# Preparing a chunked RWKV-7 scan: products of one engine given to another, and decays read one column to the left

## The chip, the cores and the metric

One NeuronCore of a Trainium2 chip runs the whole program in one launch. Its engines work side by side, each through its own queue in order: TensorE (PE, matrix products), VectorE (DVE), ScalarE (ACT), GpSimd (POOL) and SyncE (SP), which only issues the transfers here. An instruction waits at the head of its queue until the semaphores it names are reached. The metric is the device time of one execution in microseconds (us), as the median of a few runs.

## The reference, cut to what matters

The program computes two blocks. The first is a modulated norm, an input projection, two mixers (retention and RWKV-7, both run forward and backward over time), an output projection and a mixture of 16 experts; the second has two layers of attention-like mixers and a feed-forward part. The change touches only the preparation of the RWKV-7 scan of the first block, for 256 tokens and 256 context tokens, eight heads of 64 channels:

```
def decay(wl, w0_d, w2_d):
    w_log = -jax.nn.softplus(-(w0_d + jnp.tanh(wl) @ w2_d)) - 0.5
    return heads(jnp.exp(-jnp.exp(w_log)))
iclr = jax.nn.sigmoid(a0 + al @ a2)
kk = heads(k * k_k)
kk = kk / jnp.maximum(jnp.linalg.norm(kk, axis=-1, keepdims=True), 1e-12)
k_mod = heads(k * (1.0 + (iclr - 1.0) * k_a))
...
    sa = jnp.einsum('bhvk,bhk->bhv', S, a_t)
    S = S * w_t[:, :, None, :] + sa[..., None] * b_t[:, :, None, :] + v_t[..., None] * k_t[:, :, None, :]
    return S, jnp.einsum('bhvk,bhk->bhv', S, r_t)
```

with `a = -kk` and `b = kk * iclr`.

## The kernel before, in words

**The scan in chunks.** The kernel takes the scan in chunks of 64 tokens. In a chunk the decays become running products, so the kernel sums their logarithms along the chunk (`pf`, a scan on DVE, L678), takes exponentials of the sums on ACT, and multiplies keys, rates and read vectors with them. The results are two kinds of tiles: `AX` (what is read: `a` and `r` with their decay) and `BK` (what is written: `k` and `b` with the inverse decay). Both exist for `part` 1 (context) and `part` 0 (tokens), in the order's names `ax1`/`ax0` and `bk1`/`bk0`; which pair of channel blocks they belong to is told by a number. Channels come in four blocks `b` of 128; directions are `d`.

**`rwkv_decay`** (L665 to L687) runs twice with two blocks each: for b = 0 and 1 at 131 to 150 us, for b = 2 and 3 at 207 to 226 us. For each direction it computes the log decay `lw` (ACT L676, DVE L677), its running sum `pf` (DVE L678), on GpSimd the sum without a token's own decay, `lw = pf - lw` (L679), and five exponentials on ACT (L685 to L687), some of `pf` and some of the new `lw`. All the exponentials of one direction stand in one row on the ACT queue, and behind the last of them stand the roundings `wh` (L346) of the next weights of the input projection.

**Weights.** The projection runs in three passes per weight tile `w`: ACT rounds it to `wh` (L346), DVE computes the rest `wl = w - wh` (L348, every twelfth piece on POOL), and PE multiplies both. So PE waits for ACT and DVE where these two are busy with something else.

**`rwkv_prep`** (L690 to L750) computes, for one block, the normed key `av` (the last step is L726), the tile `KB` that holds `b` and the modified key (L730 on POOL for the head e = 0 and on DVE for e = 1), the bonus (L734, L738), and then multiplies the exponentials in place: `AX` by `av` (L744), `BK` by `KB` (L748) and `AX`'s second row by the read vector `rc` (L750). For part 1 the first two are on DVE, for part 0 on POOL; L750 is always on POOL. Two blocks are woven with each other and with the projection that gives the next blocks' inputs: b = 0, 1 at 228 to 262 us (round 1), b = 2, 3 at 262 to 298 us (round 2). `AF.Ln` (L711) and the functions `Exp` and `Tanh` (L719, L702) need different tables of ACT, hence the table loads.

**After that** come the scores (`rwkv_scores`, which begin with ACT L779), the inverse of a triangular matrix for the context, all on DVE (`rwkv_inverse` with `part` 1, L823 and L825), and the one for the tokens on POOL. Of the 32 scores of the tokens, the first 16 are masked on POOL (`mask`, L1346), while DVE works on the first inverse. `R.marks` holds DVE's instructions of that inverse, in order. Then come the scan's steps, the output projection and the experts, whose weights SP begins to fetch as soon as tiles of the steps are free (L1594, L1617).

The order of each queue is made when the program is built: the instructions are written by hand in interleaved generators (`weave`), and a scheduler with modelled durations picks the order, `later` giving some a delay and `issue_after` naming an instruction behind which others may be picked.

Of the kernel before, what the change touches and what calls it, by code (L numbers as in the profile page):

```python
# [11 lines left out]
AF = mybir.ActivationFunctionType  # L12
OP = mybir.AluOpType
AX = mybir.AxisListType
# [242 lines left out]
LY = 200  # L257
VM = [(1, 3, 5, 7), (1, 3, 5, 7)]
M1 = 20
NM = 16  # L260
LOW = 17
PLAN = "40044420644644006046040420666,26425,0,42,0,,,,140,1005,100,,10,,,303,3,,31,,,,3,3,3530"
# [4 lines left out]
class K:  # L267
# [39 lines left out]
    def col(s, n, i=None):  # L307
        o, w = s.at["col"][n]
        return s.colt[:, o:o + w] if i is None else s.colt[:, o + i:o + i + 1]
# [111 lines left out]
def ch(a):  # L421
    return a.rearrange("p (c t) -> p c t", t=64)


def hsl(h):
    return slice(64 * (h % 2), 64 * (h % 2) + 64)


def c64(h):
    return slice(64 * h, 64 * h + 64)  # L430


def c128(i):
    return slice(128 * i, 128 * i + 128)
# [133 lines left out]
def later(k, n):  # L568

    return k.tc.high_priority(offset=-n)  # L570
# [28 lines left out]
def weave(*gens):  # L599

    gens = list(gens)
    while gens:
        for g in list(gens):
            if next(g, gens) is gens:
                gens.remove(g)
# [33 lines left out]
def rwkv_in(k, R, bb, hT, m, own=None):  # L639

    S = k.S
    n, cw = ((512, "cw_k"), (1024, "cw_v"), (0, "cw_r"))[m]
    w = wcols(k, RW + n + 256 * bb)
    nt = 256 if m == 2 else 512
    for b in range(2):
        p = dense_t(k, w, 128 * b, 128, hT, nt)
        x = own[:, nt * b:nt * b + nt] if own is not None else k.t([128, nt], *(None, k.tq, ("rc", 2))[m])
        conv3(k, p, cw, 2 * bb + b, x)  # L650
        if m == 1:
            if bb == b == 1:
                yield
            with later(k, LC):
                p = k.ps("pr")
                for j in range(4):
                    k.mm(p[:, c128(j)], x[:, c128(j)], k.tab("cen"))
                S.activation(R.v[:, :, c128(2 * bb + b)], p.rearrange("p (j n) -> p j n", j=4), AF.Copy)
                p = k.ps("pr")
                for i in range(2):  # L660
                    k.mm(p[:, 2 * i:2 * i + 2], x[:, c128(i)], k.tab("hsel"))
                S.activation(R.mean[:, :, 4 * bb + 2 * b:4 * bb + 2 * b + 2],
                             p[:, :4].rearrange("p (i c) -> p i c", i=2), AF.Copy, scale=1.0 / 64)
        yield x


def rwkv_decay(k, R, b):

    V, G, S = k.V, k.G, k.S
    pt = lambda a, part: ch(a[:, 256 * part:256 * part + 256])  # L670
    ps = [k.ps("pr") for _ in range(2)]
    k.beside(*[(ps[d], R.w2[c64(d), c128(b)], R.wl[c64(d), :]) for d in range(2)])
    for d in range(2):
        p = ps[d]
        lw, pf = k.t([128, 512], *k.tq), k.t([128, 512], *k.tq)
        S.activation(lw, p, AF.Tanh, scale=0.5, bias=R.hw[:, 4 * d + b:4 * d + b + 1])  # L676
        V.tensor_scalar(lw, lw, -0.5 * DECAY, -0.5 * DECAY, op0=OP.mult, op1=OP.add)  # L677
        V.tensor_tensor_scan(pf, R.rs, lw, 0.0, op0=OP.mult, op1=OP.add)  # L678
        G.tensor_tensor(lw, pf, lw, op=OP.subtract)  # L679
        S.activation(R.WC[:, d, :, b], ch(pf)[:, :, 63], AF.Exp)  # L680

        fa, fb, sg = (lw, pf, 1.0) if d == 0 else (pf, lw, -1.0)
        for part in (1, 0):
            AX, BK = R.AX[part][b // 2][:, d, b % 2], R.BK[part][b // 2][:, d, b % 2]
            S.activation(AX[:, :, 0, :], pt(fa, part), AF.Exp, scale=sg)  # L685
            S.activation(BK, pt(fb, part)[:, :, None, :].to_broadcast([128, 4, 2, 64]), AF.Exp, scale=-sg)
        S.activation(R.AX[0][b // 2][:, d, b % 2, :, 1, :], pt(fb, 0), AF.Exp, scale=sg)  # L687


def rwkv_prep(k, R, b, kc, rc):  # L690


    V, G, S, col = k.V, k.G, k.S, k.col
    q2 = lambda n=512: k.t([128, 512], *k.tq)[:, :n]
    bs = c128(b)
    pt = lambda a, part: ch(a[:, 256 * part:256 * part + 256])

    with later(k, LP):
        p = k.ps("pr")
        k.mm(p, R.a2[:, bs], R.al)  # L700
        thi = q2()
        S.activation(thi, p, AF.Tanh, scale=0.5, bias=R.hw[:, 8 + b:9 + b])  # L702
    with later(k, LQ):
        rn = q2()
        S.activation(rn, kc, AF.Square, scale=col("k_k", b))
        p = k.ps("pr")
        k.mm(p, k.tab("bones"), rn)
    yield
    with later(k, LQ):
        V.tensor_scalar(rn, p, 1e-24, None, op0=OP.max)  # L710
    S.activation(rn, rn, AF.Ln)  # L711
    km = q2()
    if AC & 1:
        S.activation(km, thi, AF.Identity, scale=R.ka[:, b:b + 1], bias=R.ka[:, 4 + b:5 + b])
    else:
        V.tensor_scalar(km, thi, R.ka[:, b:b + 1], R.ka[:, 4 + b:5 + b], op0=OP.mult, op1=OP.add)
    V.tensor_tensor(km, km, kc, op=OP.mult)
    yield
    S.activation(rn, rn, AF.Exp, scale=-0.5)  # L719
    if AC & 2:  # L720
        S.activation(thi, thi, AF.Copy, scale=-0.5, bias=-0.5)
    else:
        V.tensor_scalar(thi, thi, -0.5, -0.5, op0=OP.mult, op1=OP.add)
    yield
    av = rn
    V.scalar_tensor_tensor(av, kc, R.ka[:, 8 + b:9 + b], rn, op0=OP.mult, op1=OP.mult)  # L726
    yield
    KB = k.t([128, 8, 2, 64], "kb", 2)
    for e in range(2):
        (G, V)[e].tensor_tensor(KB[hsl(e), :, e, :], ch(thi)[hsl(e)], ch(av)[hsl(e)], op=OP.mult)  # L730
        S.activation(KB[hsl(e), :, 1 - e, :], ch(km)[hsl(e)], AF.Copy)
    yield
    pr = q2(256)
    V.scalar_tensor_tensor(pr, rc, col("r_k", b), km[:, :256], op0=OP.mult, op1=OP.mult)  # L734
    p = k.ps("py")
    for i in range(2):
        k.mm(p[:, 2 * i:2 * i + 2], pr[:, c128(i)], k.tab("hsel"))
    V.tensor_copy(R.bonus[:, :, 2 * b:2 * b + 2], p[:, :4].rearrange("p (i c) -> p i c", i=2))  # L738
    for part, E in ((1, V), (0, G)):
        for d in range(2):  # L740
            yield
            AX, BK = R.AX[part][b // 2][:, d, b % 2], R.BK[part][b // 2][:, d, b % 2]
            x = AX[:, :, 0, :]
            E.tensor_tensor(x, x, pt(av, part), op=OP.mult)  # L744
            S.activation(AX[hsl(1), :, 2 - part, :], x[hsl(1)], AF.Copy)
            if part:
                G.memset(x[hsl(1)], 0.0)
            E.tensor_tensor(BK, BK, KB[:, 4 * part:4 * part + 4], op=OP.mult)  # L748
            if part == 0:
                G.tensor_tensor(AX[:, :, 1, :], AX[:, :, 1, :], ch(rc), op=OP.mult)  # L750


def rwkv_scores(k, R, part, d, todo):
# [486 lines left out]
def stage1(k, x, m, mod2, gt2, wr):  # L1240
# [3 lines left out]
    V, G, S = k.V, k.G, k.S  # L1244
# [7 lines left out]
    R = Rwkv()  # L1252
# [50 lines left out]
    with ExitStack() as st:  # L1303
        k.pool = p1 = k.tmp
        ret = k.pool = k.open(st, "s1r")
        k.load_tab(4)
        retention(k, hT, latT, 0)
        k.pool = k.tmp
        rwkv_lora(k, R, hT)
        for b in range(2):  # L1310
            rwkv_decay(k, R, b)
        k.pool = ret
        retention(k, hT, latT, 1)
    heads(k.open(left, "s1h1"))
    k.pool = k.tmp
    for bb in range(2):
        rwkv_decay(k, R, 2 + bb)
    for _ in k.fill:
        pass
    kc, rc = list(rwkv_in(k, R, 0, hT, 0, gt2)), list(rwkv_in(k, R, 0, hT, 2))  # L1320
    kc2, rc2 = [], []
    weave(*[rwkv_prep(k, R, b, kc[b], rc[b]) for b in range(2)],
          itertools.chain((kc2.append(z) for z in rwkv_in(k, R, 1, hT, 0, x[:, :1024])),
                          (rc2.append(z) for z in rwkv_in(k, R, 1, hT, 2, R.rs))))
    tail = rwkv_in(k, R, 1, hT, 1, gt2)
    weave(*[rwkv_prep(k, R, 2 + b, kc2[b], rc2[b]) for b in range(2)],
          itertools.chain(rwkv_in(k, R, 0, hT, 1), itertools.islice(tail, 2)))
    proj.close()
# [15 lines left out]
    def mask(todo):  # L1344
        for t, w in todo:
            G.tensor_tensor(t, t, w, op=OP.mult)  # L1346

    todo = []
# [8 lines left out]
    todo = []  # L1357
    lat = itertools.chain(rwkv_scores(k, R, 0, 0, todo), rwkv_scores(k, R, 0, 1, todo))
    last = modulation(2, k.t([128, 512], "modr", 2), "pm", "pr", lambda: k.w(2, 512))
    weave(itertools.islice(last, 17), lat)  # L1360
    inv = rwkv_inverse(k, R, 0, G, R.marks[M1])
    mask(todo[:NM])
    next(inv)

    def masks():
        for i in range(NM, 32, 2):
            for t, w in todo[i:i + 2]:
                V.tensor_tensor(t, t, w, op=OP.mult)
            yield
# [969 lines left out]
```

## Time and profile before

| | before |
|---|---|
| median of 3 runs, lowest and highest | 1673.66 us, 1672.74 to 1674.38 |
| the profiled execution: time, span of the trace | 1671.39 us, 1669.5 us |
| mean granted TensorE clock | 0.918 of full speed |
| busy: PE, DVE, ACT, POOL | 1383.8, 811.6, 644.7, 241.5 us |
| POOL instructions | 311 |

The span runs from the first to the last recorded instruction, and 1.89 us of the execution's time lie around it. A busy share is a mean over stages with very different limits: the first block's mixers, where the change is, end at about 475 us, and the experts that follow wait for their weights. So what counts here is what the engines wait for between 130 and 300 us. PE's granted clock is given as a share of full speed (1.00 is 2.4 GHz, 0.50 is 1.2 GHz; a share between them is a mean over the stretch).

### The profile page before, as it was taken

What the parts mean: (1) busy time and instruction counts of PE and PEld (TensorE: products, weight loads), DVE (VectorE), ACT (ScalarE), POOL (GpSimd) and SP (SyncE); (2) the same over time, 40 slices, a digit from 0 to 9 for tenths busy, and PEclk for the clock granted to TensorE, in tenths of its full rate; (3) what the DMA queues carried; (4) which work ended last, traced back from release to release, by engine and by line L of the source; (5) the groups of instructions that cost most, each with busy time, mean ns of one, the idle gap of its engine ahead of it and who ended that gap; (6) DMA issues with size and microseconds to landing.
All of it is one profiled execution on the core that took longest, in us unless ns stands there. A gap on an engine that the chain in (4) does not pass through costs nothing.

```text
span 1669.5 us, 28499 instructions
## 1 busy us (share of the span) xinstructions
PE 1383.8 (83%) x11695; PEld 1052.0 (63%) x11695; DVE 811.6 (49%) x1874; ACT 644.7 (39%) x1527; POOL 241.5 (14%) x311
## 2 busy tenths in 40 slices
PE   6899987878878675656555699889999999899998
PEld 2778865445644332322222387779999988789997
DVE  2455578797541000000000368875556578765564
ACT  3345475754421010100000357554444356444443
POOL 1222344653510000000000111200000022100000
PEclk9999998979879787877877899989999999999999
DMA  9642310703569999999999742355555132345552
GB/s 340 209 150 82 104 51 13 248 13 108 202 276 386 426 427 427 426 426 427 426 427 425 287 163 77 102 214 217 186 193 177 48 132 87 114 152 179 198 177 103
DMA packets 48194, 368.27 MB, mean 221 GB/s; under 512 B 5888, under 2 KB 7552, under 8 KB 23488
## 3 DMA queue, kind: packets, MB, share of 16 engines
q1 hardware_dynamic: 48064, 366.45, 57.2%
q8 instruction: 92, 1.51, 0.4%
q14 instruction: 38, 0.31, 0.1%
HBM read 365.38 MB, written 1.05 MB: 219 GB/s over the span
## 4 chain that ended last, share of the span: by engine, by line
PE 45%; DMA 25%; DVE 14%; ACT 4%; issue 2%; POOL 1%; DVEq 0%; POOLq 0%; SPq 0%; ACTq 0%
PE pd L383 23%; DMA w<-in_w_gu_dram 14%; PE pa L383 12%; DMA w<-in_w_down_dram 9%; PE pm L383 3%; PE c L383 2%; PE pr L383 2%; PE py L383 1%; DVE wl L348 1%; DMA w<-in_w_t_dram 1%; DVE x L825 1%; ACT wh L346 1%; DVE at L844 1%; DVE gs L823 1%; DVE x L2116 1%
## 5 line engine op out<-in xcount | busy, mean ns | idle before, releaser
L348 DVE TENSOR_TENSOR wl<-w,wh 128x512 fp32r<-128x512 f32 (+4 forms) x480 | 306.0, 674 | 147.6 <-ACT wh L346 145.7
L346 ACT ACTIVATE wh<-w 128x512 fp32r<-128x512 f32 (+5 forms) x492 | 263.2, 594 | 169.2 <-PE pa L383 52.6
L383 PE MATMUL pd<-b,wh 128*128 128x256 f32 (+1 forms) x1760 | 319.9, 282 | 0.1
L383 PEld LDWEIGHTS pd<-b,wh 128*128 128x128 f32 (+1 forms) x1760 | 271.1, 187 | 4.6 <-issue 1.1
L383 PE MATMUL pd<-w,b 128*32 128x256 f32 x2048 | 161.5, 472 | 104.9 <-DMA w<-in_w_gu_dram 102.5
L383 PE MATMUL pd<-b,wl 128*128 128x256 f32 (+1 forms) x880 | 247.4, 281 | 1.2 <-DVE wl L348 1.1
L383 PEld LDWEIGHTS pd<-w,b 128*32 128x32 f32 x2048 | 73.6, 130 | 191.1 <-DMA w<-in_w_gu_dram 108.3
L1604 DVE SCALAR_TENSOR_TENSOR th<-th,pd 128x256 f32<-128x256 f32 x16 | 6.7, 421 | 376.1 <-ACT th L1603 376.1
L383 PEld LDWEIGHTS pd<-b,wl 128*128 128x128 f32 (+1 forms) x880 | 164.4, 187 | 3.0 <-DVE wl L348 1.6
L402 POOL TENSOR_TENSOR st<-st,half 128x1 f32<-128x1 f32 (+1 forms) x20 | 17.0, 849 | 845.0 <-DVE st L457 829.1
L383 PE MATMUL pa<-wh,hd 128*128 128x512 f32 x352 | 117.5, 398 | 0.0
L383 PE MATMUL pd<-w,hd 128*32 128x256 f32 x1024 | 87.1, 500 | 26.2 <-DMA w<-in_w_down_dram 20.4
L1603 ACT ACTIVATE th<-pd 128x256 f32<-128x256 f32 x16 | 6.1, 383 | 251.1 <-PE pd L383 251.1
L383 PEld LDWEIGHTS pd<-w,hd 128*32 128x32 f32 x1024 | 39.2, 137 | 68.4 <-DMA w<-in_w_down_dram 24.0
L383 PE MATMUL pd<-wh,b 128*128 128x256 f32 (+2 forms) x320 | 77.4, 328 | 4.2 <-ACT wh L346 3.8
L383 PEld LDWEIGHTS pa<-wh,hd 128*128 128x128 f32 x352 | 64.8, 188 | 16.7 <-DVE hd L2168 3.0
L1624 ACT ACTIVATE ye<-pd 32x256 f32<-32x256 f32 x64 | 24.0, 374 | 126.8 <-PE pd L383 126.2
L383 PE MATMUL pa<-wl,hd 128*128 128x512 f32 x176 | 69.0, 392 | 0.0
L383 PEld LDWEIGHTS pd<-wh,b 128*128 128x128 f32 x320 | 55.2, 196 | 8.5 <-ACT wh L346 4.3
L383 PE MATMUL pd<-wl,b 128*128 128x256 f32 (+2 forms) x160 | 52.4, 328 | 0.6 <-DVE wl L348 0.4
L2131 ACT ACTIVATE q<-pd 128x256 f32<-128x256 f32 x44 | 16.5, 376 | 73.3 <-PE pd L383 73.3
L383 PE MATMUL pm<-hi,wh 128*128 128x256 f32 (+1 forms) x120 | 41.8, 349 | 1.6 <-ACT hi L1236 1.3
(538 smaller groups left out, 2596.2 us busy)
## 6 DMA issues: line engine op xcount, KB each, us to landing
w<-in_w_gu_dram SPq DMA_DIRECT2D x64, 2048.0 KB, 39.2
w<-in_w_down_dram SPq DMA_DIRECT2D x31, 2048.0 KB, 39.2
w<-in_w_down_dram SPq DMA_DIRECT2D x24, 1024.0 KB, 4.9
w<-in_w_gate_dram SPq DMA_DIRECT2D x22, 1024.0 KB, 5.0
w<-in_w_up_dram SPq DMA_DIRECT2D x22, 1024.0 KB, 4.9
w<-in_w_in_dram SPq DMA_DIRECT2D x34, 512.0 KB, 3.7
w<-in_w_mod_dram SPq DMA_DIRECT2D x29, 512.0 KB, 6.5
w<-in_w_t_dram SPq DMA_DIRECT2D x14, 1024.0 KB, 4.8
```

Source lines behind the costliest of these rows:

```text
L346: s.S.activation(out[0][:, c], w[:, c], AF.Copy)
L348: (s.V, s.G)[s.sc % s.every == 0].tensor_tensor(out[1][:, c], w[:, c], out[0][:, c], op=OP.subtract)
L383: s.pe = s.P.matmul(out, lhsT, rhs, start=start, stop=stop, skip_group_check=shared).ins
L402: s.G.tensor_tensor(out, ms, s.half[:, :ms.shape[-1]], op=OP.pow)
L823: F.tensor_tensor(t, M[:, a:b, j:j + 1].to_broadcast(sh), M[:, j:j + 1, :j].to_broadcast(sh), op=OP.mult)
L825: R.marks.append(F.tensor_tensor(M[:, a:b, :j], M[:, a:b, :j], t, op=OP.add).ins)
L844: V.transpose(AT[d][64 + 32 * h:96 + 32 * h].rearrange("p c h t -> p t (c h)")[:, a[h], :], m)
L1603: S.activation(th, pg, AF.Tanh, scale=0.5)
L1604: V.scalar_tensor_tensor(th, th, 1.0, pg, op0=OP.add, op1=OP.mult)
L1624: S.activation(ye[32 * e:32 * e + 32, 256 * j:256 * (j + 1)], p[32 * j:32 * j + 32], AF.Copy)
L2116: k.V.tensor_tensor(x[i][:, sl], p, x[i][:, sl], op=OP.add)
L2131: S.activation(o, p[0], AF.Tanh, scale=0.5)
```

## The change

It has three parts. First, in `rwkv_decay` the subtraction on GpSimd is gone. An exponential of the sum without a token's own decay is the exponential of the same running sum `pf`, read one column to the left: columns 1 to 63 of the output are taken from columns 0 to 62 of `pf`, and column 0 is set to 1 by a memset on GpSimd. The number of exponentials stays at five a direction and block; 20 memsets are new and 8 subtractions are gone. Second, in `rwkv_prep` all products go to DVE. Third, the first 16 masks of the token scores are put behind the last mark of the context's inverse with `issue_after`.

```
+M2 = -1
...
-        G.tensor_tensor(lw, pf, lw, op=OP.subtract)
         S.activation(R.WC[:, d, :, b], ch(pf)[:, :, 63], AF.Exp)
-
-        fa, fb, sg = (lw, pf, 1.0) if d == 0 else (pf, lw, -1.0)
+        sg = 1.0 - 2.0 * d
+
+        def factor(out, part, scale, own):
+            lf = pt(pf, part)[:, :, None, :]
+            sh = [128, 4, out.shape[2], 64 if own else 63]
+            if own:
+                S.activation(out, lf.to_broadcast(sh), AF.Exp, scale=scale)
+            else:
+                G.memset(out[:, :, :, 0:1], 1.0)
+                S.activation(out[:, :, :, 1:], lf[:, :, :, :63].to_broadcast(sh), AF.Exp, scale=scale)
         for part in (1, 0):
...
-            S.activation(AX[:, :, 0, :], pt(fa, part), AF.Exp, scale=sg)
-            S.activation(BK, pt(fb, part)[:, :, None, :].to_broadcast([128, 4, 2, 64]), AF.Exp, scale=-sg)
-        S.activation(R.AX[0][b // 2][:, d, b % 2, :, 1, :], pt(fb, 0), AF.Exp, scale=sg)
+            factor(AX[:, :, 0:1, :], part, sg, d == 1)
+            factor(BK, part, -sg, d == 0)
+        factor(R.AX[0][b // 2][:, d, b % 2, :, 1:2, :], 0, sg, d == 0)
...
-        (G, V)[e].tensor_tensor(KB[hsl(e), :, e, :], ch(thi)[hsl(e)], ch(av)[hsl(e)], op=OP.mult)
+        V.tensor_tensor(KB[hsl(e), :, e, :], ch(thi)[hsl(e)], ch(av)[hsl(e)], op=OP.mult)
...
-    for part, E in ((1, V), (0, G)):
+    for part in (1, 0):
...
-            E.tensor_tensor(x, x, pt(av, part), op=OP.mult)
+            V.tensor_tensor(x, x, pt(av, part), op=OP.mult)
...
-            E.tensor_tensor(BK, BK, KB[:, 4 * part:4 * part + 4], op=OP.mult)
+            V.tensor_tensor(BK, BK, KB[:, 4 * part:4 * part + 4], op=OP.mult)
             if part == 0:
-                G.tensor_tensor(AX[:, :, 1, :], AX[:, :, 1, :], ch(rc), op=OP.mult)
+                V.tensor_tensor(AX[:, :, 1, :], AX[:, :, 1, :], ch(rc), op=OP.mult)
...
-    mask(todo[:NM])
+    with k.tc.issue_after(R.marks[M2]):
+        mask(todo[:NM])
```

Line numbers of the changed kernel are 1 larger in the helpers (L349 for L348), and 11 larger from L688 on (L755 for L744).

On POOL's queue, in round 1 of the preparation, stood before:

```order
L348 TENSOR_TENSOR wl_2236<-w_2233,wh_2235 128x256
L730 TENSOR_TENSOR kb_2397<-q_364_2207,q_365_2209 64x8x64
L744 TENSOR_TENSOR ax_76_336<-ax_76_336,q_365_2209 128x4x64 x2
L730 TENSOR_TENSOR kb_2402<-q_368_2215,q_369_2217 64x8x64
L744 TENSOR_TENSOR ax_76_336<-ax_76_336,q_369_2217 128x4x64 x2
L750 TENSOR_TENSOR ax_331_1984<-ax_331_1984,m_65 128x4x64
L748 TENSOR_TENSOR bk_77_337<-bk_77_337,kb_2397 128x512 x2
L750 TENSOR_TENSOR ax_331_1984<-ax_331_1984,m_65 128x4x64
L748 TENSOR_TENSOR bk_77_337<-bk_77_337,kb_2402 128x512 x2
L348 TENSOR_TENSOR wl_2470<-w_2467,wh_2469 128x256
L750 TENSOR_TENSOR ax_331_1984<-ax_331_1984,m_65 128x4x64 x2
L747 MEMSET ax_74_334 64x4x64 x4
```

and in the changed kernel, from the last decay's memsets on, the queue through both rounds is:

```order
L691 MEMSET bk_332_1991 128x8
L691 MEMSET ax_331_1990 128x4
L349 TENSOR_TENSOR wl_2248<-w_2245,wh_2247 128x256
L349 TENSOR_TENSOR wl_2482<-w_2479,wh_2481 128x256
L758 MEMSET ax_74_334 64x4x64 x4
L349 TENSOR_TENSOR wl_2610<-w_2607,wh_2609 128x256
L758 MEMSET ax_329_1988 64x4x64 x4
```

All that reads tiles on POOL between 226 and 297 us is now three `wl` pieces; the rest are memsets.

On DVE's queue, the end of round 1 was, in front of the `wl` pieces for which PE waits:

```order
L738 COPY bonus_80<-py_2415 128x2x2
L744 TENSOR_TENSOR ax_74_334<-ax_74_334,q_365_2209 128x4x64
L748 TENSOR_TENSOR bk_75_335<-bk_75_335,kb_2397 128x512
L744 TENSOR_TENSOR ax_74_334<-ax_74_334,q_369_2217 128x4x64
L748 TENSOR_TENSOR bk_75_335<-bk_75_335,kb_2402 128x512
...
L348 TENSOR_TENSOR wl_2470<-w_2467,wh_2469 128x256 x2
```

(the two pairs stand there twice, for the two directions), and in the changed kernel the same eight products are followed by eight for part 0 (`ax_76`, `bk_77`):

```order
L755 TENSOR_TENSOR ax_74_334<-ax_74_334,q_369_2229 128x4x64
L759 TENSOR_TENSOR bk_75_335<-bk_75_335,kb_2414 128x512
L755 TENSOR_TENSOR ax_76_336<-ax_76_336,q_365_2221 128x4x64
L759 TENSOR_TENSOR bk_77_337<-bk_77_337,kb_2409 128x512
L755 TENSOR_TENSOR ax_76_336<-ax_76_336,q_369_2229 128x4x64
L759 TENSOR_TENSOR bk_77_337<-bk_77_337,kb_2414 128x512
...
L349 TENSOR_TENSOR wl_2482<-w_2479,wh_2481 128x256 x3
```

So 16 products instead of 8 stand ahead of these `wl`, and ahead of them four `KB` products (L741) instead of two.

On ACT's queue, round 2 had its table loads (of L711, L702, L711, L719) spread over two blocks, one block after the other:

```order
L711 ACT_TABLE_LOAD
L711 ACTIVATE q_397_2455<-q_397_2455 128x512
L702 ACT_TABLE_LOAD
L702 ACTIVATE q_400_2461<-pr_2459,hw_1065 128x512
L705 ACTIVATE q_401_2463<-x_64,colt_60 128x512
...
L719 ACTIVATE q_397_2455<-q_397_2455 128x512
...
L711 ACT_TABLE_LOAD
L711 ACTIVATE q_401_2463<-q_401_2463 128x512
```

and in the changed kernel both blocks stand together, with two loads:

```order
L716 ACTIVATE q_401_2475<-x_64,colt_60 128x512
...
L722 ACT_TABLE_LOAD
L722 ACTIVATE q_397_2467<-q_397_2467 128x512
...
L722 ACTIVATE q_401_2475<-q_401_2475 128x512
L730 ACT_TABLE_LOAD
L730 ACTIVATE q_397_2467<-q_397_2467 128x512
L730 ACTIVATE q_401_2475<-q_401_2475 128x512
```

In round 1 there are two loads in both kernels, but the first load no longer stands behind a rounding and a convolution (L346, L530).

The masks (`sr` and `ax0`) with what they wait for are, before and of the change in this order:

```order
L1346 TENSOR_TENSOR ax_76_336<-ax_76_336,tab_9_75 64x4x64 [waits Activation_49]
L1346 TENSOR_TENSOR sr_2992<-sr_2992,tab_9_75 128x4x64 [waits Activation_49,Pool_49]
L1346 TENSOR_TENSOR ax_76_336<-ax_76_336,tab_9_75 64x4x64 [waits Activation_49]
L1346 TENSOR_TENSOR sr_2992<-sr_2992,tab_9_75 128x4x64 [waits Activation_49]
L1346 TENSOR_TENSOR ax_76_336<-ax_76_336,tab_9_75 64x4x64 [waits Activation_49,Pool_49]
```

```order
L1357 TENSOR_TENSOR ax_76_336<-ax_76_336,tab_9_75 64x4x64 [waits Activation_49]
L1357 TENSOR_TENSOR sr_3004<-sr_3004,tab_9_75 128x4x64 [waits Activation_49,Pool_49]
L1357 TENSOR_TENSOR ax_76_336<-ax_76_336,tab_9_75 64x4x64 [waits Activation_49]
L1357 TENSOR_TENSOR sr_3004<-sr_3004,tab_9_75 128x4x64 [waits Activation_49]
L1357 TENSOR_TENSOR ax_76_336<-ax_76_336,tab_9_75 64x4x64 [waits Activation_49,Pool_49]
```

They stand at the same place of POOL's queue, after the last memset of the score tiles and ahead of POOL's inverse, and all 16 wait for ACT and POOL alone in both kernels.

## Rows read from the trace of the kernel before

**Rows 1.** Windows: length, busy PE, PEld, DVE, ACT, POOL; PE's clock, DMA share, GB/s.
```profile
250.00:258.00 8.00, 0.00 (x0) 0.00 (x0) 7.97 (x6) 1.35 (x5) 7.40 (x8) 0.59 0.00 0
...
152.00:156.00 4.00, 4.00 (x19) 3.82 (x20) 2.79 (x7) 0.31 (x2) 1.52 (x2) 0.57 0.65 161
225.00:228.00 3.00, 3.00 (x9) 2.37 (x9) 0.43 (x1) 3.00 (x8) 1.61 (x3) 0.57 0.01 3
```

**Rows 2.** ACT's waits, 131 to 150 us: us in total, times, longest.
```profile
ACT ax L685 <- POOL q L679: 1.4, 2, 0.7
ACT bk L686 <- POOL q L679: 1.4, 2, 0.8
```

**Rows 3.** ACT's waits, 205 to 227 us.
```profile
ACT bk L686 <- POOL q L679: 2.3, 2, 1.4
ACT ax L685 <- POOL q L679: 1.0, 2, 0.6
```

**Rows 4.** PE's waits, 148 to 152 us.
```profile
PE pm L383 <- ACT wh L346: 1.7, 1, 1.7
PE pm L383 <- DVE wl L348: 0.7, 2, 0.4
```

**Rows 5.** PE's waits, 220 to 228 us.
```profile
PE c L383 <- DVE wl L348: 2.9, 2, 2.4
```

**Rows 6.** Timeline of PE at the end of round 1; in brackets the idle time before.
```profile
259.70 1.22 PE L383 MATMUL c<-ax,bk 128*128 128x128 f32 x4 [12.80 <-POOL ax L747]
261.48 0.80 PE L383 MATMUL pm<-hi,wl 128*128 128x512 f32 x1 [0.56 <-DVE wl L348]
```

**Rows 7.** Timeline of DVE, the same place.
```profile
252.91 4.78 DVE L744 TENSOR_TENSOR ax<-ax,q 128x256 f32<-128x256 f32 x1
257.61 0.68 DVE L748 TENSOR_TENSOR bk<-bk,kb 128x512 f32<-128x512 f32 x1
258.21 0.41 DVE L744 TENSOR_TENSOR ax<-ax,q 128x256 f32<-128x256 f32 x1
258.54 0.68 DVE L748 TENSOR_TENSOR bk<-bk,kb 128x512 f32<-128x512 f32 x1
...
261.02 1.08 DVE L348 TENSOR_TENSOR wl<-w,wh 128x256 fp32r<-128x256 f32 x3
```

**Rows 8.** Timeline of POOL, its last two products of round 1.
```profile
256.01 1.39 POOL L750 TENSOR_TENSOR ax<-ax,m 128x256 f32<-128x256 f32 x2
```

**Rows 9.** DVE's groups, 242 to 262 us: busy us, mean ns, idle before.
```profile
L730 DVE TENSOR_TENSOR kb<-q,q 64x512 f32<-64x512 f32 x2 | 6.3, 3171 | 0.1
...
L726 DVE SCALAR_TENSOR_TENSOR q<-gt,ka,q 128x512 f32<-128x512 f32 x2 | 2.8, 1416 | 1.5 <-ACT q L719 1.5
```

**Rows 10.** DVE's groups, 279.5 to 297 us.
```profile
L748 DVE TENSOR_TENSOR bk<-bk,kb 128x512 f32<-128x512 f32 x4 | 4.3, 1082 | 0.0
L734 DVE SCALAR_TENSOR_TENSOR q<-m,colt,q 128x256 f32<-128x256 f32 x2 | 3.8, 1910 | 0.0
L730 DVE TENSOR_TENSOR kb<-q,q 64x512 f32<-64x512 f32 x2 | 3.5, 1771 | 0.1
L744 DVE TENSOR_TENSOR ax<-ax,q 128x256 f32<-128x256 f32 x4 | 3.2, 792 | 0.0
```

**Rows 11.** The chain that ended last, a piece of round 2.
```profile
270.08 1.28 ACT L702
```

**Rows 12.** POOL's groups, 0 to 60 us: a small memset.
```profile
L621 POOL MEMSET m<- 128x8 f32 x1 | 0.1, 117 | 0.1
```

**Rows 13.** POOL's groups, 120 to 400 us.
```profile
L1346 POOL TENSOR_TENSOR ax<-ax,tab 64x256 f32<-64x256 f32 x16 | 11.7, 728 | 7.0 <-ACT ax L792 5.0 <-PE pr L383 1.1 <-POOL mean L1000 0.6
...
L748 POOL TENSOR_TENSOR bk<-bk,kb 128x512 f32<-128x512 f32 x8 | 10.6, 1342 | 0.0
```

**Rows 14.** SP's waits before the experts' weights, 395 to 945 us.
```profile
SPq L1594 <- PE pd L383: 53.7, 11, 26.9
```

## The prediction

> **What bounds the kernel now.** The change lies between 130 and 300 us, so I read that stretch: PE's waits first, then the engines that it waits for, then what stretches their work.
>
> PE has three kinds of gap there. At the end of the first decay it waits for the roundings `wh` and then for `wl` [rows 4]; at the end of the second for `wl` again [rows 5]; at the end of round 1 it stands still for 12.80 us and 0.56 more [rows 6]. The last waiter there is `wl` at 261.02, which stands on DVE's queue behind the products of the preparation [rows 7]. In 250 to 258 us PE does nothing, while DVE is busy for 7.97 of 8.00 us and POOL for 7.40 [rows 1].
>
> What is DVE busy with? The same product L744 takes 4.78 us at 252.91 and 0.41 at 258.21, with the same shape [rows 7]. The long one ends at 257.69, and POOL's run of products ends at 257.40 (256.01 and 1.39) [rows 8]. L748 takes 0.68 behind that point [rows 7], and 1.082 on average in round 2, beside POOL's products [rows 10]. So DVE's products with two SBUF inputs are held up as long as POOL runs such products, and PE stands behind them. Round 2 shows the same on L734 and L730 [rows 10].
>
> **The change, part by part.** Prices first: behind each other and undisturbed, an AX product (128x256) costs 258.54 - 258.21 = 0.33 us and a BK product (128x512) 258.21 - 257.61 = 0.60 [rows 7]. `KB` has as many columns as BK, so 0.60; L750 has AX's, so 0.33. L726 and L734 have a scalar operand as well, but 512 and 256 columns, and I take 0.70 and 0.40 for them, a little above the products. 28 products come over to DVE: 4 KB, 8 AX, 8 BK, 8 with `rc`. POOL loses them and the 8 subtractions.
>
> *First decay.* ACT loses four waits for the subtraction, 1.4 + 1.4 = 2.8 us [rows 2]; the exponentials stay as many, and 63 columns for 64 give nothing. So `wh` comes 2.8 us earlier or more (DVE's small scaling L677 runs beside POOL too). PE loses 1.7 + 0.7 = 2.4 us of waiting [rows 4], and behind the gap its clock is low: 0.57 of full speed in a stretch of 4.00 us without a pause [rows 1], in which 4.00 x 0.43 = 1.7 us are the clock's. PE can thus regain 2.4 to 4.1 us, if ACT follows. I take **3.6**.
>
> *Second decay.* ACT loses 2.3 + 1.0 = 3.3 us of waits [rows 3], PE 2.9 [rows 5] and of the slow 3.00 us behind it 3.00 x 0.43 = 1.3 [rows 1]: 2.9 to 4.2. Four `rc` products, 1.3 us, now stand on DVE between the second and the third `wl` piece; the third waits for ACT's exponentials anyway. I take **3.6**, and 2.9 - 1.3 = 1.6 as the floor.
>
> The memsets: one of 128x8 takes 0.117 us [rows 12], 20 are 2.3. They stand on POOL's queue long before the exponentials that follow them, behind memsets that were there already, and POOL then only waits; I take nothing. Without that cover, if the ten of one decay came last, they would cost up to 1.2 us each time.
>
> *Round 1.* On DVE ahead of `wl`, the two KB shrink from 3.171 to 0.60, 5.1 us [rows 9]; the first AX from 4.70 (252.91 to 257.61) to 0.33, 4.4 [rows 7]; the two L726 from 2.83 to 1.40, 1.4 [rows 9]: 10.9 in all. Added are 2 KB, 4 AX and 4 BK: 1.2 + 1.3 + 2.4 = 4.9. That leaves 6.0. L726 also idles 1.5 us for ACT's L719 [rows 9], whose first table load now starts two ACT instructions earlier; I count a third of it. **6.5**, with bounds of 5.2 (if the ten added products cost their full 0.41 and 0.68, 0.08 more each, and the idle stays) and 7.5.
>
> Which part of a stretch is POOL's? The 4.78 us run on until POOL's last product ends, through several of them [rows 7, 8]. The Trainium skill, page "SBUF — State Buffer", section "Who interferes with whom", states that of a GpSimd instruction and a DVE one with two SBUF inputs the one that starts first holds the shared port pair for its whole length, and the other is blocked until it finishes. By that rule the trace agrees on which instructions collide, but one wait for one POOL instruction would be too short for 4.78 us; the sum by the rows is 6.5 here, and by the rule 1.0 (the first rival).
>
> *Round 2.* By the same prices, L748 gives 4 x (1.082 - 0.60) = 1.9, L744 4 x (0.792 - 0.33) = 1.8, L730 2 x (1.771 - 0.60) = 2.3 and L734 2 x (1.910 - 0.40) = 3.0 [rows 10]: 9.0, less the same 4.9 added, 4.1. The four `rc` products of this round fall where DVE has nothing to do (behind the burst of `wl` at its start). The load at 270.08 lies on the chain that ends last, 1.28 us [rows 11], and goes. 4.1 to 5.4; I take **4.8**.
>
> *Masks.* They keep their place and wait for ACT and POOL alone, as before; no wait on DVE is built. Marking them changes nothing that runs: **0**. POOL's 16 masks, 11.7 us [rows 13], still run beside DVE's inverse. SP's queue is in the same order as before, so no transfer is moved past another.
>
> *Behind it.* Scores, inverses, steps and the experts follow in a chain. SP's loads of the experts' weights wait for PE to release tiles, 53.7 us in eleven waits, the longest 26.9 [rows 14], so they start earlier by as much.
>
> Sum: 3.6 + 3.6 + 6.5 + 4.8 = 18.5 us. The profiled execution took 1671.39, so it would take 1652.9; the median of the runs is 2.27 higher, 1673.66, and gives **1655.2 us**.
>
> **The rivals.**
>
> *A DVE instruction waits for one POOL instruction at most.* Then of a stretch no more than one POOL product, 1.34 us at the longest mean [rows 13], would be POOL's, and the rest has another cause and stays: of the two KB of round 1 2 x (3.17 - 0.60 - 1.34) = 2.5, of the AX 4.37 - 1.34 = 3.0, of L734 in round 2 up to 3.0 - 1.34 = 1.7. The gain falls by 7.2 to 11.3, the time is 1662.4. Against it: the 4.78 us end with POOL's whole run, not with one product. Chance 0.10.
>
> *The decays' gain is swallowed.* If the projection's next weights come no earlier, PE runs into them and the two decays give nothing: 18.5 - 7.2 = 11.3 us are left, again 1662.4. For it: a transfer is issued only when its tile is free, and PE has no pause behind the first decay [rows 1] that could show how much slack there is. Against: that release follows the `wl` three tiles before, which moves too. Chance 0.12.
>
> *The masks do wait.* Then DVE's inverse is free of them, which is worth at most their 11.7 us [rows 13], and they run behind it, ahead of POOL's own inverse, which can take that gain back. What is left between 0 and 11.7 I put at a quarter, 3 us: 1652.2. Chance 0.05, since the built order shows no such wait.
>
> *Slower: the stretch isn't POOL's.* If DVE's two-input products are slow there for another reason (ACT reads and writes the same tiles), nothing of the 10.9 + 9.0 comes back. Then the rounds cost 2 x 4.9 more, less 0.5 and 1.3 for the table loads: 8.0 lost against 7.2 won, 1674.5, no change. And if the added products are stretched like those of round 2 (4 x 1.082 + 4 x 0.792 + 2 x 1.771 = 11.0 a round), 20.2 are lost against 7.2: 1686.7. It decides from the point at which the ten of a round cost more than (7.2 + 1.8) / 2 = 4.5 us while the old stretch stays. Against: the short rows stand behind POOL's run with ACT as busy as before. Chance 0.05 for slower, 0.04 for no change.
>
> *The shift ends at the experts.* Their weights come as a stream for hundreds of us; if it starts by something else than PE's release, the time stays at 1673. Against it are SP's waits [rows 14]. Chance 0.04.
>
> **How the numbers follow.** The forecast has 0.60: all four terms hold, within their bounds. The lower ends are 2.4, 1.6, 5.2 and 4.1, 13.3 in all, and the upper 4.1, 4.2, 7.5 and 5.4, 21.2; all at one end at once is unlikely, so the likeliest case's own range is 1652 to 1661. The range takes in the two cases at 1662 and the masks: 1650 to 1664, which leaves out the rest. A change below 0.2% (3.3 us) can hardly be told from none here. Faster: 0.60 + 0.10 + 0.12 + 0.05 = 0.87. The same: 0.04 + 0.04 = 0.08. Slower 0.05.
>
> **What would show it.** Right: no ACT wait for POOL at L692; PE's gaps at 148 and 221 us gone and its clock full there; DVE's L755 and L759 at 0.41 and 0.68 throughout; PE's stop in round 1 near 6 us instead of 13; two table loads in round 2; masks still beside DVE's inverse, which is as long as before; all later stages 18 us earlier. Wrong: long products on DVE without POOL beside them (the last rival), a PE that waits for `w` at 160 to 200 us, or an experts' stage that starts at the same time.

## The result, and the profile after

The changed kernel took **1652.62 us** (median of 6 runs) against 1672.53 us for the kernel before in the same session (6 runs, 1670.66 to 1674.38). The ratio is 0.988, with a 95% interval of 0.9868 to 0.9893: 1.07 to 1.32% faster, 20.1 us by the ratio, where the sum had 18.5. In one execution of the changed kernel, the profiled one, most of TensorE's matmuls ran 2.3 to 2.7 times as long (4386.37 us); it counts in this median but not in the ratio, and the rows of "after" come from a second run of the identical kernel: 1649.43 us (6 runs, 1646.56 to 1657.13) against 1670.63 (11 runs), ratio 0.9878 (0.9859 to 0.9897), span of the trace 1644.8 us against 1669.5, mean clock 0.923 against 0.918.

Windows of the changed kernel (columns as in [rows 1]): the ends of the two decays, the end of round 1, and a part of the scan's steps that comes up later.

```profile
148.00:152.00 4.00, 4.00 (x34) 3.95 (x33) 4.00 (x9) 2.18 (x8) 1.98 (x3) 1.00 0.26 60
216.00:221.00 5.00, 5.00 (x20) 3.28 (x19) 3.46 (x10) 4.91 (x14) 0.74 (x1) 1.00 0.00 2
238.00:247.00 9.00, 7.82 (x16) 3.66 (x16) 8.94 (x21) 6.80 (x16) 1.23 (x4) 0.62 0.00 0
368.00:392.00 24.00, 19.59 (x432) 12.58 (x432) 20.81 (x29) 8.04 (x19) 3.01 (x7) 1.00 0.48 126
```

At both decays PE is now busy all the time, at full clock; the waits of [rows 4, 5] and the slow stretches behind them [rows 1] are gone. ACT's waits from 131 to 150 us, its two largest, against [rows 2]:

```profile
ACT wc L680 <- DVE q L679: 1.2, 2, 1.0
ACT wh L347 <- PE pm L384: 0.6, 1, 0.6
```

It no longer waits for POOL. DVE's timeline at the end of round 1, against [rows 7]:

```profile
239.22 0.43 DVE L755 TENSOR_TENSOR ax<-ax,q 128x256 f32<-128x256 f32 x1
239.56 0.69 DVE L759 TENSOR_TENSOR bk<-bk,kb 128x512 f32<-128x512 f32 x1
240.17 0.42 DVE L755 TENSOR_TENSOR ax<-ax,q 128x256 f32<-128x256 f32 x1
...
246.12 0.69 DVE L759 TENSOR_TENSOR bk<-bk,kb 128x512 f32<-128x512 f32 x1
246.72 0.42 DVE L349 TENSOR_TENSOR wl<-w,wh 128x256 fp32r<-128x256 f32 x1
```

Sixteen products take 246.72 - 239.22 = 7.50 us; the eight of before took 8.11 (252.91 to 261.02 [rows 7]). PE's waits from 233 to 260 us, against the 12.80 and 0.56 of [rows 6]:

```profile
PE pr L384 <- ACT q L716: 1.1, 1, 1.1
PE pm L384 <- DVE wl L349: 0.9, 1, 0.9
```

DVE's groups in round 2, 258 to 278 us, against [rows 10]:

```profile
L759 DVE TENSOR_TENSOR bk<-bk,kb 128x512 f32<-128x512 f32 x8 | 5.5, 685 | 0.0
L755 DVE TENSOR_TENSOR ax<-ax,q 128x256 f32<-128x256 f32 x8 | 3.4, 419 | 0.0
L741 DVE TENSOR_TENSOR kb<-q,q 64x512 f32<-64x512 f32 x4 | 2.7, 684 | 0.1
...
L745 DVE SCALAR_TENSOR_TENSOR q<-m,colt,q 128x256 f32<-128x256 f32 x2 | 0.9, 480 | 0.0
```

Twice as many products in about the time of before; L745, which is L734 of before, fell from 1910 to 480 ns. Over the whole span DVE is busy for 801.5 us instead of 811.6, with 28 products more: so its busy time of before must have held time in which it was only kept waiting. ACT's table loads from 233 to 280 us, one of each where round 2 alone had four:

```profile
L722 ACT ACT_TABLE_LOAD x1 | 1.3, 1283 | 0.0
L730 ACT ACT_TABLE_LOAD x1 | 1.3, 1283 | 0.0
```

Four places of the program, in us from the start of the span, for this kernel and for the parts tried below (a row each; the last column is the span):

| | PE back at work after round 1 | first score on ACT | token inverse begins on POOL | first `w_gu` fetched by SP | span |
|---|---|---|---|---|---|
| before | 261.48 | 296.50 | 352.11 | 412.16 | 1669.5 |
| the change | 247.20 | 277.11 | 332.54 | 391.65 | 1644.8 |
| decays alone | 252.60 | 289.89 | 345.93 | 409.15 | 1661.9 |
| products alone | 256.20 | 287.58 | 343.62 | 404.98 | 1660.5 |
| change, masks do wait | 246.31 | 278.23 | 328.54 | 391.03 | 1645.8 |
| change, half of BK on POOL | 248.36 | 282.97 | 338.38 | 398.23 | 1650.8 |
| change, half of KB on POOL | 247.84 | 276.95 | 332.34 | 392.78 | 1649.7 |

### The profile page after: what moved, and what is told of

Same layout as the page of the kernel before. It is cut to its first block, busy times and chain, and to the rows that moved or that the text cites. A ratio compares the mean times of both kernels' runs of the same rounds, so it can differ in the third digit from the quotient of the medians.

```text
span 4384.6 us, 28502 instructions
## 1 busy us (share of the span) xinstructions
PE 4294.5 (98%) x11695; PEld 2901.6 (66%) x11695; DVE 795.1 (18%) x1902; ACT 647.4 (15%) x1525; POOL 200.5 (5%) x295
## 4 chain that ended last, share of the span: by engine, by line
PE 97%; DVE 1%; issue 1%; ACT 0%; POOL 0%; DMA 0%; SPq 0%; DVEq 0%; POOLq 0%; ACTq 0%
PE pd L384 48%; PE pa L384 20%; PE pm L384 11%; PE c L384 8%; PE pr L384 5%; PE py L384 4%; PE pa L396 1%; PE pd L396 1%; PE pr L396 1%; PE pa L1960 0%; DVE th L1617 0%; DVE th L1618 0%; DVE hd L1623 0%; ACT th L1616 0%; DVE xn L1246 0%
## 5 line engine op out<-in xcount | busy, mean ns | idle before, releaser
L384 PE MATMUL pd<-b,wh 128*128 128x256 f32 (+1 forms) x1760 | 959.2, 674 | 0.0
L384 PEld LDWEIGHTS pd<-b,wh 128*128 128x128 f32 (+1 forms) x1760 | 852.2, 563 | 39.5 <-issue 33.6
L384 PE MATMUL pd<-b,wl 128*128 128x256 f32 (+1 forms) x880 | 600.4, 683 | 0.0
L384 PEld LDWEIGHTS pd<-b,wl 128*128 128x128 f32 (+1 forms) x880 | 492.9, 560 | 14.1 <-issue 12.5
L349 DVE TENSOR_TENSOR wl<-w,wh 128x512 fp32r<-128x512 f32 (+4 forms) x480 | 300.2, 662 | 877.4 <-ACT wh L347 854.0
L384 PE MATMUL pd<-w,b 128*32 128x256 f32 x2048 | 424.5, 1099 | 0.6 <-DVE b L1593 0.6
L384 PE MATMUL pa<-wh,hd 128*128 128x512 f32 x352 | 339.6, 1071 | 0.0
L384 PE MATMUL pd<-wh,b 128*128 128x256 f32 (+2 forms) x320 | 221.3, 806 | 2.4 <-ACT wh L347 2.4
L384 PE MATMUL pd<-w,hd 128*32 128x256 f32 x1024 | 211.3, 1093 | 8.3 <-DVE hd L1623 7.8
L384 PE MATMUL pa<-wl,hd 128*128 128x512 f32 x176 | 188.2, 1070 | 0.0
L384 PE MATMUL pm<-hi,wl 128*128 128x256 f32 (+1 forms) x120 | 103.9, 868 | 0.0
```

The source lines that it names most:

```text
L349: (s.V, s.G)[s.sc % s.every == 0].tensor_tensor(out[1][:, c], w[:, c], out[0][:, c], op=OP.subtract)
L384: s.pe = s.P.matmul(out, lhsT, rhs, start=start, stop=stop, skip_group_check=shared).ins
```

## The experiments

All were timed in five rounds beside the kernel before; gains and losses are by the ratios. The theory is the prediction's: POOL's products hold up DVE's two-input instructions, and PE stands behind them; the decays give their part separately. Its rivals were that one POOL instruction is all that a DVE instruction waits for, that the decays' gain is swallowed, and that the stretch had another cause.

**The identical kernel once more.**

> The changed kernel once more, for a profile that is undisturbed. Theory (POOL's products held DVE's up, and DVE held PE up): about 1653 us, 19 to 20 less than before; the products L755 and L759 take 0.41 and 0.68 us everywhere in both rounds, PE's stop in round 1 is 6 to 7 us shorter than 12.8, the ACT waits for POOL in the decays are gone with PE's pauses behind them, and the masks still run beside DVE's inverse, which is as long as before (stretched for about 15 us). Rival (one POOL product held a DVE instruction for 1.34 us at most): some products on DVE stay at 1.5 us or more with no POOL product beside them.

Measured 1649.43 us, ratio 0.9878 (above). The gain of the first session is confirmed. None of DVE's products L755 and L759 is longer than 0.69 us in either round, so the rival's products of 1.5 us and more are not there.

**The decays alone**: the kernel before with the new `rwkv_decay`.

```
-        G.tensor_tensor(lw, pf, lw, op=OP.subtract)
+            factor(AX[:, :, 0:1, :], part, sg, d == 1)
+            factor(BK, part, -sg, d == 0)
...
```

> The kernel before with the new rwkv_decay alone. Theory: the two decays give 3.6 us each, 7.2 in all, so about 1665.4 against 1672.5 before (bounds 4 to 8.3 us of gain). Rival (the gain is swallowed in the PE-bound stretch behind): under 2 us of gain. The preparation's long products (L744 near 4.8 us in this trace's round 1) stay, since POOL keeps them.

Measured 1663.98 us, ratio 0.9963 (0.9949 to 0.9977): 6.2 us faster, 7.2 expected. DVE's groups of its round 2, 262 to 290 us:

```profile
L758 DVE TENSOR_TENSOR bk<-bk,kb 128x512 f32<-128x512 f32 x4 | 4.7, 1186 | 0.0
L744 DVE SCALAR_TENSOR_TENSOR q<-m,colt,q 128x256 f32<-128x256 f32 x2 | 3.8, 1916 | 0.0
L740 DVE TENSOR_TENSOR kb<-q,q 64x512 f32<-64x512 f32 x2 | 3.6, 1776 | 0.1
L754 DVE TENSOR_TENSOR ax<-ax,q 128x256 f32<-128x256 f32 x4 | 3.2, 797 | 0.0
```

The stretch of [rows 10] is all there (1186 for 1082, 1916 for 1910, 1776 for 1771, 797 for 792 ns), so the decays have nothing to do with it. PE's stop in round 1 is as long as before (12.75 us for 12.80). And the decays' gain is not swallowed: PE comes out of round 1 8.9 us earlier.

**The products alone**: the kernel before with the new `rwkv_prep`.

```
-    for part, E in ((1, V), (0, G)):
+    for part in (1, 0):
...
```

> The kernel before with the new rwkv_prep alone. Theory: rounds 1 and 2 give 6.5 and 4.8 us, 11.3 in all, so about 1661.2 against 1672.5 before (bounds 9 to 13). Rival (the stretch of DVE's products isn't POOL's doing): 8 us slower, 1680. The decays' ACT waits for POOL stay (about 2.8 and 3.3 us).

Measured 1664.12 us, ratio 0.9962 (0.9949 to 0.9976): 6.4 us faster (4.0 to 8.5), where 11.3 were expected of it, with bounds of 9 and 13. The sign and the place are right (the first score comes 8.9 us earlier), the size is not. PE's waits from 220 to 258 us:

```profile
PE c L383 <- DVE wl L348: 3.2, 1, 3.2
PE pr L383 <- ACT q L705: 2.9, 2, 1.9
PE pm L383 <- DVE wl L348: 1.6, 1, 1.6
```

The first is the second decay's, which this kernel leaves as it was [rows 5]. Of round 1 it gets 5.3 us for 6.8 in the full change, of round 2 (PE back at work to the first score) 35.02 - 31.38 = 3.6 for 5.1.

**The masks do wait.** To make the change's third part real, the 16 masks read a copy of their table that DVE makes at the end of the context's inverse; the computation stays the same.

```
+    R.scm = k.t([128, 256], "scm2")
+    V.tensor_scalar(R.scm, k.tab("scm"), R.ym[:, 1, 0, 0:1], None, op0=OP.mult)
...
-    scm = k.tab("scm")
+    scm = R.scm if lat else k.tab("scm")
```

> The changed kernel with 16 masks that really wait: they read a copy of the mask table that DVE makes near the end of its inverse (one DVE instruction more). The masks are no input of that inverse. Theory (POOL's reads hold DVE's two-input products up): the stretch of 314 to 330 us before is gone, and DVE's inverse is 7 to 8 us shorter; of that some 2 to 4 us reach the end, since POOL's own inverse must wait for the masks then: about 1650 against 1653. Rival 1 (the stretch has another cause): inverse as long as before, time the same or up to 4 us longer. Rival 2 (POOL's inverse starts later than before for the masks): DVE's inverse shorter, time 2 to 5 us longer.

Measured 1650.98 us, ratio 0.988 (0.9863 to 0.9896), the same as the change. The transposes around DVE's inverse of the context:

```profile
294.51 1.93 DVE L817 STREAM_TRANSPOSE x<-at 64x1024 f32<-64x1024 f32 x1
...
315.23 1.93 DVE L817 STREAM_TRANSPOSE x<-at 64x1024 f32<-64x1024 f32 x1
```

From one to the other 20.7 us. The same two in the changed kernel, and then in the kernel before:

```profile
293.44 1.94 DVE L817 STREAM_TRANSPOSE x<-at 64x1024 f32<-64x1024 f32 x1
...
321.58 1.91 DVE L817 STREAM_TRANSPOSE x<-at 64x1024 f32<-64x1024 f32 x1
```

```profile
313.58 1.93 DVE L806 STREAM_TRANSPOSE x<-at 64x1024 f32<-64x1024 f32 x1
...
341.67 1.90 DVE L806 STREAM_TRANSPOSE x<-at 64x1024 f32<-64x1024 f32 x1
```

Both take 28.1 us. So POOL's 16 masks beside it, which give that inverse nothing to read, cost it 7.4 us: this shows by intervention that POOL's products slow DVE's. POOL's four memsets of round 1 do not: they lie between 240 and 244 us in the changed kernel, where DVE's products stay at 0.42 and 0.69 us. POOL's own inverse begins 4.0 us earlier, and yet the first `w_gu` comes only 0.6 us earlier and the time stays, where 2 to 4 us less were expected. In between, the steps ran at a lower clock:

```profile
365.00:391.00 26.00, 22.76 (x433) 13.97 (x434) 21.12 (x30) 8.44 (x20) 2.31 (x4) 0.87 0.42 117
```

That window, from behind POOL's inverse to the first `w_gu`, has a clock of 0.87 here and 1.00 in the change. That the clock took the 4 us back is likely, but read from one profile of each.

**Half of the BK products back on POOL**: eight products of part 0.

```
-            V.tensor_tensor(BK, BK, KB[:, 4 * part:4 * part + 4], op=OP.mult)
+            (G, V)[part].tensor_tensor(BK, BK, KB[:, 4 * part:4 * part + 4], op=OP.mult)
```

> The change with the eight products of the second half of BK (part 0, 128x512) back on GpSimd, four in each round; the new decays stay. If GpSimd's products hold DVE's two-input instructions for as long as their run lasts: GpSimd takes 4 x 1.34 = 5.4 us a round, DVE is relieved of 4 x 0.69 = 2.7 and held for up to 5.4, so the time is that of the change up to 5 us more, 1649 to 1655, and the trace has single DVE products of 2 us and more that end with GpSimd's run. If the stretch in the kernel before had another cause: DVE keeps 0.69 and 0.42 for each, and each round is 2.7 us shorter, 1644. If a DVE instruction waits for one GpSimd instruction at most: none is longer than 0.69 + 1.34 = 2.0 us, and the time is within 3 us of the change.

Measured 1657.07 us, ratio 0.9921 (0.9907 to 0.9935): about 7 us slower than the change, though DVE has eight products fewer. This is more than any theory had, though the intervals of the two ratios do not exclude the 5 us of the first. DVE's and then POOL's timeline in round 1:

```profile
237.54 1.67 DVE L741 TENSOR_TENSOR kb<-q,q 64x512 f32<-64x512 f32 x1
239.24 0.23 DVE L749 COPY bonus<-py 128x4 f32<-128x4 f32 x2
239.48 1.13 DVE L755 TENSOR_TENSOR ax<-ax,q 128x256 f32<-128x256 f32 x1
240.53 1.75 DVE L759 TENSOR_TENSOR bk<-bk,kb 128x512 f32<-128x512 f32 x1
242.21 1.49 DVE L755 TENSOR_TENSOR ax<-ax,q 128x256 f32<-128x256 f32 x1
243.62 0.68 DVE L759 TENSOR_TENSOR bk<-bk,kb 128x512 f32<-128x512 f32 x1
```

```profile
236.89 6.53 POOL L759 TENSOR_TENSOR bk<-bk,kb 128x512 f32<-128x512 f32 x4 [2.30 <-DVE kb L741]
```

From 243.62 on, 0.2 us behind POOL's run, all of DVE's products are short again: the stretch is POOL's, which ends the rival of another cause. But here the two engines seem to take turns, each DVE product behind one product of POOL (6.53 / 4 = 1.63 us), and none is longer than 1.75; on this point the expectation of 2 us and more was wrong, and these lengths fit the theory of one instruction at most, but its time (within 3 us of the change) does not. Of the 5.9 us by which the first score is later than in the change, round 1 loses 1.2 (248.36 for 247.20) and round 2 loses 4.7: it takes 282.97 - 248.36 = 34.6 us for 29.9. A row of PE's timeline there:

```profile
275.61 2.50 PE L384 MATMUL pr<-tab,gt 128*128 128x128 f32 x12 [3.64 <-DVE gt L534]
```

PE waits 3.64 us for DVE, which reaches L534 late, behind the products that POOL's second run (266.67 to 272.93 us) stretches; and then its twelve matmuls take 2.50 us, for 1.40 in the change; the clock from 272 to 283 us is 0.84.

**Half of the KB products back on POOL**: the four with e = 0.

```
-        V.tensor_tensor(KB[hsl(e), :, e, :], ch(thi)[hsl(e)], ch(av)[hsl(e)], op=OP.mult)
+        (G, V)[e].tensor_tensor(KB[hsl(e), :, e, :], ch(thi)[hsl(e)], ch(av)[hsl(e)], op=OP.mult)
```

> The change with the first of the two KB products of each pair (64x512) back on GpSimd, two in each round, where they stood in the kernel before. Neither is followed at once by another GpSimd product. If a run of GpSimd's products is what holds DVE: a single product of 1.32 us holds one DVE instruction for up to 1.3 us and relieves DVE of 0.68, so each pair costs up to 0.6 us, 1.3 a round, and the time is 1649 to 1652, not to be told from the change; in the trace the other KB product (L741) is about 1.3 us long instead of 0.68 and the products of BK and AX stay at 0.69 and 0.42. If the 3.17 us of the KB product in the kernel before had been its own cost beside ACT's copies, it shows here again with 2 to 3 us in round 1, and the time is 1654 or more.

Measured 1650.03 us, ratio 0.9876 (0.9859 to 0.9892): the change's own time, as expected. DVE, then POOL, in round 1:

```profile
234.87 1.61 DVE L741 TENSOR_TENSOR kb<-q,q 64x512 f32<-64x512 f32 x1
...
237.00 0.69 DVE L741 TENSOR_TENSOR kb<-q,q 64x512 f32<-64x512 f32 x1
```

```profile
233.96 1.28 POOL L741 TENSOR_TENSOR kb<-q,q 64x512 f32<-64x512 f32 x1 [0.63 <-DVE q L737]
235.20 0.72 POOL L349 TENSOR_TENSOR wl<-w,wh 128x256 fp32r<-128x256 f32 x1
```

The KB product beside POOL takes 1.61 us, where about 1.3 was expected, its twin 0.69. It ends at 236.48, 0.56 us behind POOL's `wl`, so it sat through the rest of POOL's KB and all of the `wl`: two instructions of POOL's run, not one. The 3.17 us of [rows 9] are thus not this product's own cost.

## Why the prediction was right, point by point

**The decays: 3.6 + 3.6 were forecast, 7.5 came.** An instruction on ACT behind the first decay, L1124 of before, moved from 190.51 to 187.10 us (3.4 from the first decay), and the two `wh` behind the second from 226.02 to 218.53: 7.5 in all, 4.1 of it from the second. Alone, the decays gave 6.2 us at the end. The 20 memsets cost nothing that shows: no instruction of ACT waits for POOL at the exponentials.

**Round 1: 6.5 forecast, 6.8 measured** (PE back at work 14.3 us earlier, less 7.5). The prices held from start to start: a pair of products takes 0.94 us (7.50 / 8), where 0.33 + 0.60 was taken. What the text said of PE's stop, near 6 us instead of 13, came out otherwise: PE stands for 1.10 and 0.92 us only, since other matmuls now lie in the gap, but these run at a clock of 0.62 (238 to 247 us). The stop became slow work, and its end moved as forecast. How the 14.3 us divide depends on what is taken out first: alone, the decays moved PE's return by 8.9 us and the products by 5.3, just over their lower bound of 5.2.

**Round 2: 4.8 forecast, 5.1 measured** (35.02 us from PE's return to the first score before, 29.91 after), but in part by luck. Round 2 in the kernel before, the change, the decays alone and the products alone (columns as in [rows 1]):

```profile
261.50:296.50 35.00, 32.88 (x164) 26.22 (x164) 27.73 (x42) 21.39 (x42) 13.33 (x14) 0.95 0.15 49
```

```profile
247.20:277.10 29.90, 29.51 (x162) 24.63 (x162) 28.00 (x59) 15.96 (x32) 4.54 (x8) 1.00 0.18 57
```

```profile
252.60:289.90 37.30, 34.48 (x156) 27.21 (x157) 28.66 (x41) 21.57 (x42) 14.03 (x15) 0.90 0.08 25
```

```profile
256.20:287.60 31.40, 30.86 (x158) 25.41 (x160) 27.40 (x58) 15.74 (x33) 3.49 (x8) 0.92 0.19 63
```

The sum counted what DVE and a table load give back. PE's idle time falls only from 2.1 to 0.4 us, though; its busy time falls by 3.4. Of these, about 1.9 are the clock's, as an estimate: in the kernel before it was 0.59 in the first 4.52 us behind PE's stop (4.52 x 0.41), and in the change it is 1.00 from PE's return on. And the matmuls `pr<-q,tab` (twice) and `pr<-x`, 3.2 us in round 2 before (from 267.64 us on), now run in round 1's gap (238.46 to 246.28 us): the order of the queues changed with the products, and this was not tried by itself. How the 3.4 us are made up of the two was not followed further; neither was a term of the sum. Alone, the products gave 3.6, below the lower bound of 4.1.

**The masks: 0 forecast.** No run has the change without this part, so the 0 is not measured by itself; but the inverse beside them takes 28.1 us before and after, and the masks run beside it as before. The 11.7 us of [rows 13] are 16 `ax` masks, eight of which belong to the context's scores; the 16 masks meant here are eight `ax` and eight `sr`, 11.9 us in the kernel before, so that figure was near by chance. That a real wait would bring little was right in its size, but for another reason than the one given: POOL's inverse did begin 4.0 us earlier, and the steps behind it took that back, probably by their clock.

**The rivals.** *At most one POOL instruction* would have left 1.0 us for round 1; 6.8 came. The Trainium skill, page "SBUF — State Buffer", section "Who interferes with whom", has the first starter hold the shared ports for its whole instruction while the other is blocked. By that rule the traces agree on who collides, and the turns of the kernel with half of BK on POOL look just like it; but the 4.78 us of [rows 7] and the 1.61 above go through several POOL instructions, where the measurement decides. Which of the two forms appears was not settled. *The decays' gain is swallowed* fell with the decays alone, *the masks do wait* with the masks in the trace (294 to 319 us, beside the inverse), *the stretch isn't POOL's* with the kernels that put products back and the one whose masks wait, and *the shift ends at the experts* with the first `w_gu`, 20.5 us earlier.

**What the sum did not have.** The parts alone give 6.2 + 6.4 = 12.6 us, together 20. In the profiled executions half of the difference is there at the first score (19.4 against 6.6 + 8.9 = 15.5), and it arises in round 2: at PE's return the parts still add up (8.9 + 5.3 = 14.2 of 14.3 us). A part of it can be seen: with the decays alone, round 2 takes 37.3 us for 35.0 before, at a clock of 0.90 for 0.95; with the products alone the clock is 0.92, and in the full change 1.00. Most of the rest opens behind the start of POOL's inverse. Of the same steps the traces show, for the kernel before and then for the decays alone:

```profile
388.00:412.00 24.00, 20.77 (x398) 12.46 (x399) 20.35 (x29) 8.35 (x21) 2.54 (x5) 0.93 0.45 121
```

```profile
382.00:409.00 27.00, 23.89 (x412) 15.03 (x411) 19.56 (x26) 6.88 (x17) 2.53 (x4) 0.75 0.38 110
```

At 0.75 the decays alone lose 3.2 of their 6.2 us between the start of POOL's inverse (6.2 earlier) and the first `w_gu` (3.0 earlier); the full change, at 1.00, wins 0.9 there. But not all of this lasts to the end: the span with the decays alone is 7.6 us shorter than before, so 4.6 come back behind the first `w_gu`, where the clock is 0.96 (409 to 451 us) for 0.90 before (412 to 455 us). That these clocks explain the sizes is read from one profile of each kernel, and no run set the clock by itself: it is the likely cause, not a shown one, and how the 20 us come about from parts of 12.6 stays open in part. At 1672.5 - 12.6, about 1660 us, which is what the parts give alone, the time would still have been in the range, but above the 1655.2; that it came out below rests on what the sum did not have. The change's own runs spread over 10.6 us, those of the kernel before over 5.6.

## What to carry to other kernels

A product with two inputs in SBUF that is given to GpSimd to relieve the vector engine may cost the vector engine more than doing the product itself would: compare the same instruction beside GpSimd's run and just behind it, and count the relief only where the vector engine isn't on the path. Where two engines collide, price the stretch by the run of the other engine, and add what TensorE loses by its clock after the wait. Do not add up the gains of parts measured alone: behind each of them the granted clock of the next stage can be another.

## What the runs showed of the hardware that was not expected

**GpSimd is held too, and for longer.** In the changed kernel's trace one mask on POOL takes 9.70 us between others of 0.8:

```profile
305.04 0.76 POOL L1357 TENSOR_TENSOR sr<-sr,tab 128x256 f32<-128x256 f32 x1
306.66 9.70 POOL L1357 TENSOR_TENSOR ax<-ax,tab 64x256 f32<-64x256 f32 x1 [0.87 <-ACT ax L803]
316.44 0.80 POOL L1357 TENSOR_TENSOR sr<-sr,tab 128x256 f32<-128x256 f32 x1
```

and DVE's groups from 306 to 316 us are these two, without idle time:

```profile
L836 DVE TENSOR_TENSOR x<-x,gs 128x110 f32<-128x110 f32 (+11 forms) x27 | 6.7, 288 | 0.0
L834 DVE TENSOR_TENSOR gs<-x 128x110 f32<-128x110 f32 (+12 forms) x27 | 6.2, 267 | 0.0
```

One instruction of POOL sits through some fifty of DVE's, which stay below 0.3 us in the mean. With half of KB on POOL, a copy did the same beside a row of eight of DVE's products, and ended 0.5 us behind that row (at 274.54 us):

```profile
271.01 4.00 POOL L1351 COPY modr<-m 128x512 f32<-128x512 f32 x1
```

With half of BK on POOL that copy takes 0.61 us (279.19; DVE's row ends at 279.28). So whichever engine has an unbroken row may keep the other out for the length of the row; in other places they take turns. What decides between the two was not tried.

**The clock of the steps.** Between the end of POOL's inverse and the first `w_gu`, the same work was granted 0.75 to 1.00 of full speed in kernels that differ only in earlier stages. The fetch comes 59.1 us behind the start of POOL's inverse in the change (clock 1.00), 63.2 us with the decays alone (0.75). What sets this clock was not tried.
